# Split weights stored with the columns of eight k-tiles interleaved, in a two-layer encoder on one core

## The chip, the cores and the metric

The kernel runs on one core of one Trainium2 chip. The metric is the device time of one execution in microseconds (us), the median of the runs shown. The engines are PE (matrix multiply; its weight loads are listed apart as PEld), ACT and DVE (elementwise engines), POOL, and SP, which issues the DMAs.

## The reference

The reference is a two-layer encoder over 256 tokens with model width 2048, all in float32. Each layer is a normalisation, a projection to queries, keys and values, attention, an output projection with a residual, a second normalisation and an MLP with squared ReLU of width 8192. Cut to the matrix products, which are nearly all of the work:

```python
# layer 0: w_in (2048 x 6144); layer 1: w_qkv (2048 x 3072)
q, k, v = split(rms_norm(x, g) @ w_in)
x = x + attention(q, k, v) @ w_out                       # w_out (2048 x 2048)
h = rms_norm(x, g2)
a = relu(h @ w1)                                         # w1 (2048 x 8192)
x = x + (a * a) @ w2                                     # w2 (8192 x 2048)
...
return rms_norm(x, g_final)
```

The two attentions (a two-dimensional neighbourhood with dilated windows in layer 0, grouped heads in a band in layer 1) are small beside the products at 256 tokens.

## The kernel before, in words

**Arithmetic.** Each float32 operand of a product is split into two parts in the matmul format `float32r`: a high part `h` (the value rounded to the format) and a low part `l` (what is left). `split(hi, lo, src)` does it: ACT writes the high part (L82), then DVE subtracts it from the source and writes the low part (L83). A product is the sum of high by high, high by low and low by high.

**Tiling.** A weight matrix is cut into units of 128 output columns by 16 k-tiles of 128 rows. A unit comes in two halves of eight k-tiles (`HALF` = 8), each one DMA of 512 KB into a buffer `r` of shape [128, 8, 128] (pool `raw`, six buffers). `take_half()` issues the DMA on SP, splits the half into a tile `h` (pool `whi`) and a tile `l` (pool `wlo`), five buffers each, and runs two halves ahead of their use (`AHEAD` = 2). Both tiles have rows padded to `ROW` = 136 elements, of which 128 are used: k-tile k is a contiguous run of 128 elements, and the next begins 544 bytes further. The instructions at L82 and L83 walk k-tile after k-tile and, inside one, column after column.

**The inner loop.** `k_range` does two matmuls for each k-tile, with the weights as the stationary operand (128x128, read by the weight load) and the activations as the moving one: `h` against 512 elements, which are both parts of the activations side by side (L150), and `l` against the 256 elements of the high part (L152). All go to one accumulator `acc` in PSUM, of which there are three. The moving operand is `u` (normalised input), `o` (attention's output) or `hid` (hidden layer). In the very last unit the 512 elements are taken in two matmuls with 256 each (L147, L148).

**Around it.** Behind a unit, `joined` adds the two halves of the accumulator (ACT L179, DVE L181), and some operations of ACT and DVE on 128x256 follow, which differ by stage. The values of attention (`value_pair`, L272) use weights the other way round: there the activations are stationary and the weights, taken with `flat=True`, are the moving operand. The first unit of the first stage of a group (`some_units`, with `held` > 0) splits the last two k-tiles of a unit into small tiles `hh` and `hl` of their own (pool `held_w`, [128, 2, 128]) and multiplies them later. The first three units of the program (`STARTERS`) are loaded and split in pieces of two or four k-tiles (`GROUPS`) and multiplied at L471 and L473.

The order of the work on each engine is the order in which the code is written; attention's steps are put between the units by a list of due times (`later`, `tick`, every four k-tiles).

Of the kernel before, what the change touches and what calls it, by code (L numbers as in the profile page):

```python
# [8 lines left out]
F32R = mybir.dt.float32r  # L9
# [5 lines left out]
P = 128  # L15
# [9 lines left out]
SCALE = 128.0 ** -0.5  # L25
TW = 384
HALF = KT // 2
ROW = P + 8
RAW_BUFS = 6
PART_BUFS = 5  # L30

# [10 lines left out]
def encoder(ctx: ExitStack, tc: tile.TileContext, a: dict, outT: bass.AP):  # L42
# [4 lines left out]
    whi = ctx.enter_context(tc.tile_pool(name="whi", bufs=PART_BUFS))  # L47
    wlo = ctx.enter_context(tc.tile_pool(name="wlo", bufs=PART_BUFS))
    held_w = ctx.enter_context(tc.tile_pool(name="held_w", bufs=3))
# [31 lines left out]
    def split(hi, lo, src):  # L81
        nc.scalar.activation(hi, src, AF.Copy)  # L82
        nc.vector.tensor_sub(lo, src, hi.bitcast(F32))  # L83
# [6 lines left out]
    def need(units, held=0, flat=False):  # L90

        for i, src in enumerate(units):
            pending.extend([(src[:, :HALF, :], HALF, flat),
                            (src[:, HALF:, :], HALF - 2 if i < held else HALF, flat)])

    def take_half():
        while pending and len(loaded) <= AHEAD:
            src, n, flat = pending.pop(0)
            r = raw.tile([P, HALF, P], F32, name="r")
            nc.sync.dma_start(r, src)  # L100
            h = whi.tile([P, HALF, ROW], F32R, name="h")
            l = wlo.tile([P, HALF, ROW], F32R, name="l")
            if flat:
                h, l = (w.rearrange("p k c -> p (k c)")[:, :HALF * P] for w in (h, l))
                split(h, l, r.rearrange("p k c -> p (k c)"))
                loaded.append((h, l, None))
                continue
            h, l = h[:, :, :P], l[:, :, :P]
            split(h[:, :n, :], l[:, :n, :], r[:, :n, :])
            tiles = [(h[:, k, :], l[:, k, :]) for k in range(n)]  # L110
            if n < HALF:
                h, l = (held_w.tile([P, 2, P], F32R, name=name) for name in ("hh", "hl"))
                split(h, l, r[:, n:, :])
                tiles += [(h[:, k, :], l[:, k, :]) for k in range(2)]
            loaded.append((h, l, tiles))
        return loaded.pop(0)

    def take_unit():
        return take_half()[2] + take_half()[2]
# [65 lines left out]
    def gained(k, which):  # L185
        x, gk = xs[:, k, :], g[:, which, k:k + 1]
        if which == 4:
            nc.scalar.activation(x, x, AF.Copy, scale=gk)
        else:
            nc.scalar.activation(u[:, k, 0, :], x, AF.Copy, scale=gk)  # L190
            nc.vector.scalar_tensor_tensor(u[:, k, 1, :], x, gk, u[:, k, 0, :].bitcast(F32),
                                           op0=ALU.mult, op1=ALU.subtract)
# [68 lines left out]
    def value_pair(pool, keep):  # L261

        ps = acc_ps.tile([P, 2, T], F32, name="acc")
        for half in range(2):
            parts = [take_half()[:2] for _ in range(2)]
            for kk in range(HALF):
                k = half * HALF + kk
                h, l = (w[:, (kk % 4) * T:(kk % 4 + 1) * T] for w in parts[kk // 4])
                for j in range(2):
                    js = slice(j * P, (j + 1) * P)  # L270
                    for n, (x, y) in enumerate(((0, h), (0, l), (1, h))):
                        nc.tensor.matmul(ps[:, j, :], u[:, k, x, js], y,  # L272
                                         start=k == 0 and j == 0 and n == 0,
                                         stop=k == KT - 1 and n == 2, skip_group_check=True)
                if kk % 2 == 1:
                    tick()
        assert norm["ready"]
        w = pool.tile([P, 2, 2, T], F32R, name="v", bufs=1)
        for j in range(2):
            nc.scalar.activation(w[:, 0, j, :], ps[:, j, :], AF.Copy, scale=rcol[:, j:j + 1])  # L280
            nc.vector.scalar_tensor_tensor(w[:, 1, j, :], ps[:, j, :], rcol[:, j:j + 1],
                                           w[:, 0, j, :].bitcast(F32), op0=ALU.mult, op1=ALU.subtract)
        keep.append(w)
# [158 lines left out]
    STARTERS = 3  # L442
# [14 lines left out]
    hl = [None] * STARTERS  # L457
    for k0, k1 in GROUPS:
        ks = slice(k0 % HALF, (k1 - 1) % HALF + 1)
        if k0 % HALF == 0:  # L460
            hl = [(whi.tile([P, HALF, ROW], F32R, name="h")[:, :, :P], wlo.tile([P, HALF, ROW], F32R, name="l")[:, :, :P])
                  for _ in range(STARTERS)]
        for i in range(STARTERS):
            split(hl[i][0][:, ks, :], hl[i][1][:, ks, :], rs[k0 // HALF][i][:, ks, :])
            if i == 0:
                for k in range(k0, k1):
                    gained(k, 0)
        for i in range(STARTERS):
            h, l = hl[i]
            for k in range(k0, k1):  # L470
                nc.tensor.matmul(sps[i], h[:, k % HALF, :], u[:, k].rearrange("p a t -> p (a t)"),  # L471
                                 start=k == 0, stop=False)
                nc.tensor.matmul(sps[i][:, :T], l[:, k % HALF, :], u[:, k, 0, :], start=False, stop=k == KT - 1)  # L473
# [12 lines left out]
    with tc.tile_pool(name="attn0", bufs=1) as pool:  # L486
# [24 lines left out]
        for p in range(8):  # L511
            q, k, v = [[], []], [[], []], []
            for i in range(2):
# [6 lines left out]
                h = 2 * p + i  # L520
# [11 lines left out]
    with tc.tile_pool(name="attn1", bufs=1) as pool:  # L532
        o = pool.tile([P, NH, 2, T], F32R, name="o")
        sl = slopes(16)
        for p in range(2):
            k, v = [[], []], []
# [8 lines left out]
            for i in range(8):  # L545
                h = 8 * p + i
# [93 lines left out]
```

## Time and profile before

| | |
|---|---|
| median of 2 runs | 2112.02 us (2111.78 to 2112.26) |
| the profiled execution, its own time | 2113.29 us |
| its span, first to last instruction | 2111.4 us |
| PE busy | 2088.1 us (99%), 12438 instructions |
| PEld (weight loads) busy | 1846.7 us (87%) |
| DVE busy | 1339.8 us (63%) |
| ACT busy | 1036.6 us (49%) |
| mean granted TensorE clock | 0.995 of full speed |
| DMA | 386 MB, mean 183 GB/s |

A row of a group reads: line, engine, operation, output<-inputs, shapes and types, number of instructions | busy us in total, mean ns of one | idle time of the engine just before them, and what ended it. Matmuls overlap: a matmul's own duration is longer than the distance to the next one, so distances are read from starts in the timeline. PEld runs beside PE.

### The profile page before, as it was taken

To read this page: it belongs to the slowest core of one execution; us is meant where nothing else is said; L and a number is where in the kernel's file an instruction comes from. 1 tells how busy PE (TensorE), PEld (TensorE's weight loads), DVE (VectorE), ACT (ScalarE), POOL (GpSimd) and SP (SyncE) were. 2 spreads that over 40 slices of the span, in tenths; PEclk is the share of its full clock that TensorE was granted. 3 is DMA by queue.
4 is the path that set the end of the run, shared out by engine and by line. 5 is a ranking of instruction groups with operands and counts; after the bars stand their busy time and mean duration, and the time that the engine had idled before them with its cause. 6 is when DMAs were issued, how large, how long until landed. Compare 5 with 4: busy or idle time off the path is not lost.

```text
span 2111.4 us, 31825 instructions
## 1 busy us (share of the span) xinstructions
PE 2088.1 (99%) x12438; PEld 1846.7 (87%) x12438; DVE 1339.8 (63%) x2088; ACT 1036.6 (49%) x1602; POOL 23.0 (1%) x33
## 2 busy tenths in 40 slices
PE   8999999999999999999999999999999999999997
PEld 6999998888888888888889998888888888888887
DVE  6766676666655556666656877766665556665554
ACT  6555555544444444444445656554444434444442
POOL 2100000000000000000000000000000000000000
PEclk9999999999999999999999999999999999999999
DMA  9755555555555555555555454555555555555552
GB/s 260 176 174 167 168 174 174 191 185 189 189 188 189 189 189 189 190 189 190 189 189 185 149 163 144 190 185 188 189 189 189 189 189 189 189 189 190 189 189 91
DMA packets 108294, 386.06 MB, mean 183 GB/s; under 512 B 12352, under 2 KB 13392, under 8 KB 108144
## 3 DMA queue, kind: packets, MB, share of 16 engines
q1 hardware_dynamic: 106992, 381.73, 55.1%
q0 software_dynamic: 1008, 2.27, 1.5%
q8 instruction: 97, 1.59, 0.3%
q14 instruction: 53, 0.43, 0.1%
q10 hardware_dynamic: 144, 0.04, 0.0%
HBM read 381.89 MB, written 2.10 MB: 182 GB/s over the span
## 4 chain that ended last, share of the span: by engine, by line
PE 96%; DMA 2%; DVE 1%; ACT 0%; SPq 0%; issue 0%; DVEq 0%; ACTq 0%
PE acc L150 58%; PE acc L152 30%; PE acc L272 5%; PE s_ps L296 1%; PE m_ps L340 1%; DMA r<-in_even_w_in 1%; PE p_ps L321 1%; DMA r<-in_even_w_v 1%; DMA xs<-in_xT 0%; ACT h L82 0%; DVE l L83 0%; DVE xs L570 0%; PE acc L147 0%; PE acc L148 0%; PE m_ps L225 0%
## 5 line engine op out<-in xcount | busy, mean ns | idle before, releaser
L83 DVE TENSOR_TENSOR l<-r,h 128x1024 fp32r<-128x1024 f32 (+3 forms) x729 | 880.6, 1208 | 701.9 <-ACT h L82 699.3
L82 ACT ACTIVATE h<-r 128x1024 fp32r<-128x1024 f32 (+3 forms) x729 | 762.8, 1047 | 966.0 <-PE acc L150 635.9
L150 PE MATMUL acc<-u,h 128*128 128x512 f32 x2820 | 988.4, 394 | 0.0
L152 PE MATMUL acc<-u,l 128*128 128x256 f32 x2820 | 788.6, 280 | 0.0
L150 PE MATMUL acc<-hid,h 128*128 128x512 f32 x2016 | 702.4, 393 | 0.0
L150 PEld LDWEIGHTS acc<-u,h 128*128 128x128 f32 x2820 | 529.9, 188 | 119.2
L152 PE MATMUL acc<-hid,l 128*128 128x256 f32 x2048 | 572.3, 279 | 0.0
L152 PEld LDWEIGHTS acc<-u,l 128*128 128x128 f32 x2820 | 529.1, 188 | 0.2
L150 PEld LDWEIGHTS acc<-hid,h 128*128 128x128 f32 x2016 | 378.7, 188 | 87.3
L152 PEld LDWEIGHTS acc<-hid,l 128*128 128x128 f32 x2048 | 384.1, 188 | 0.0
L150 PE MATMUL acc<-o,h 128*128 128x512 f32 x500 | 175.2, 394 | 1.1 <-DVE z L181 1.1
L152 PE MATMUL acc<-o,l 128*128 128x256 f32 x500 | 139.8, 280 | 0.0
L272 PE MATMUL acc<-h,u 128*128 128x256 f32 x640 | 119.9, 283 | 0.0
L181 DVE TENSOR_TENSOR z<-acc,t 128x256 f32<-128x256 f32 x275 | 114.4, 418 | 2.2 <-ACT t L179 2.1
L150 PEld LDWEIGHTS acc<-o,h 128*128 128x128 f32 x500 | 93.9, 188 | 22.8 <-DVE z L181 1.7
L179 ACT ACTIVATE t<-acc 128x256 f32<-128x256 f32 x275 | 100.8, 367 | 5.5 <-PE acc L152 2.7
L272 PEld LDWEIGHTS acc<-h,u 128*128 128x128 f32 x640 | 101.1, 190 | 0.5
L152 PEld LDWEIGHTS acc<-o,l 128*128 128x128 f32 x500 | 93.8, 188 | 0.0
L272 PE MATMUL acc<-l,u 128*128 128x256 f32 x320 | 90.1, 281 | 0.0
L272 PEld LDWEIGHTS acc<-l,u 128*128 128x128 f32 x320 | 60.9, 190 | 0.1
L382 DVE SCALAR_TENSOR_TENSOR z<-z 128x256 f32<-128x256 f32 x128 | 54.2, 425 | 4.2
L83 DVE TENSOR_TENSOR hid<-z,hid 128x256 fp32r<-128x256 f32 x128 | 53.5, 419 | 1.3 <-ACT hid L82 1.2
(94 smaller groups left out, 857.6 us busy)
## 6 DMA issues: line engine op xcount, KB each, us to landing
r<-in_w_mlp_in SPq DMA_DIRECT2D x256, 512.0 KB, 4.5
r<-in_w_mlp_out SPq DMA_DIRECT2D x256, 512.0 KB, 4.5
r<-in_even_w_in SPq DMA_DIRECT2D x58, 512.0 KB, 4.2
r<-in_odd_w_qkv SPq DMA_DIRECT2D x40, 512.0 KB, 4.0
r<-in_even_w_v SPq DMA_DIRECT2D x32, 512.0 KB, 3.8
r<-in_even_w_out SPq DMA_DIRECT2D x32, 512.0 KB, 4.2
r<-in_odd_w_out SPq DMA_DIRECT2D x32, 512.0 KB, 3.8
r<-in_odd_w_v SPq DMA_DIRECT2D x8, 512.0 KB, 4.1
```

Of the source, the lines that this page charges most:

```text
L82: nc.scalar.activation(hi, src, AF.Copy)
L83: nc.vector.tensor_sub(lo, src, hi.bitcast(F32))
L150: nc.tensor.matmul(ps, h, act[:, k].rearrange("p a t -> p (a t)"), start=start, stop=False)
L152: nc.tensor.matmul(ps[:, :T], l, act[:, k, 0, :], start=False, stop=stop)
L179: nc.scalar.activation(t, ps[:, T:], AF.Copy)
L181: nc.vector.tensor_add(z, ps[:, :T], t)
L272: nc.tensor.matmul(ps[:, j, :], u[:, k, x, js], y, start=k == 0 and j == 0 and n == 0, stop=k == KT - 1 and n == 2, skip_group_check=True)
L296: nc.tensor.matmul(s_ps[:, i, :], qh[:, x, qs], kh[:, y, :], start=n == 0, stop=n == 2)
L321: nc.tensor.transpose(p_ps[:, j, i * P:(i + 1) * P], s[:, i, j * P:(j + 1) * P], ident)
L340: nc.tensor.matmul(o_ps[:, :T], vv[:, x, j, side * P:(side + 1) * P], pt[:, y, j, :], start=n == 0, stop=n == 5)
L382: nc.vector.scalar_tensor_tensor(z, z, 0.0, z, op0=ALU.max, op1=ALU.mult)
```

## The change

The tiles `h` and `l` of a half become 1024 elements without padding, and the order inside them is turned: element (k, c) stands at c * 8 + k instead of k * 136 + c. The same column of the eight k-tiles lies side by side in 32 bytes; one k-tile is 128 elements with a step of eight elements. The held tiles `hh` and `hl` are laid out the same way for their two k-tiles, with a step of two. Splits still walk k-tile after k-tile and column after column, so ACT writes `h`, and DVE reads `h` and writes `l`, with a step of eight elements; a weight load at L150, L152, L471 and L473 reads with that step. The source `r` is read contiguously as before. The `flat` tiles of the values are contiguous as before. In the built program no instruction is added, removed or moved on any engine (PE 11702 rows, DVE 1835, ACT 1297 in both): only these operands' addresses and steps differ, and the line numbers.

```diff
-ROW = P + 8
...
+    def column_major(pool, n, name):
+
+        return pool.tile([P, P * n], F32R, name=name).rearrange("p (c k) -> p k c", k=n)
...
-            h = whi.tile([P, HALF, ROW], F32R, name="h")
-            l = wlo.tile([P, HALF, ROW], F32R, name="l")
             if flat:
-                h, l = (w.rearrange("p k c -> p (k c)")[:, :HALF * P] for w in (h, l))
+                h, l = (pool.tile([P, HALF * P], F32R, name=name) for pool, name in ((whi, "h"), (wlo, "l")))
...
-            h, l = h[:, :, :P], l[:, :, :P]
+            h, l = column_major(whi, HALF, "h"), column_major(wlo, HALF, "l")
             split(h[:, :n, :], l[:, :n, :], r[:, :n, :])
             tiles = [(h[:, k, :], l[:, k, :]) for k in range(n)]
             if n < HALF:
-                h, l = (held_w.tile([P, 2, P], F32R, name=name) for name in ("hh", "hl"))
+                h, l = (column_major(held_w, 2, name) for name in ("hh", "hl"))
...
-            hl = [(whi.tile([P, HALF, ROW], F32R, name="h")[:, :, :P], wlo.tile([P, HALF, ROW], F32R, name="l")[:, :, :P])
-                  for _ in range(STARTERS)]
+            hl = [(column_major(whi, HALF, "h"), column_major(wlo, HALF, "l")) for _ in range(STARTERS)]
```

## The prediction

> **What bounds the kernel now.** I read the shares of busy time first, then the chain that ended last, then the timeline of the inner loop.
>
> ```profile
> PE 2088.1 (99%) x12438; PEld 1846.7 (87%) x12438; DVE 1339.8 (63%) x2088; ACT 1036.6 (49%) x1602; POOL 23.0 (1%) x33
> ...
> PE 96%; DMA 2%; DVE 1%; ACT 0%; SPq 0%; issue 0%; DVEq 0%; ACTq 0%
> ```
>
> PE is on the path for 96% of the span; DVE and ACT, whose splits the change touches, have 37% and 51% of the span free. So there are two questions: does the new layout alter PE's own step from matmul to matmul, and does it slow the splits so far that DVE or ACT takes PE's place? The groups give the counts and the mean durations.
>
> ```profile
> L150 PE MATMUL acc<-u,h 128*128 128x512 f32 x2820 | 988.4, 394 | 0.0
> L83 DVE TENSOR_TENSOR l<-r,h 128x1024 fp32r<-128x1024 f32 x702 | 860.6, 1226 | 688.7 <-ACT h L82 686.2
> L152 PE MATMUL acc<-u,l 128*128 128x256 f32 x2820 | 788.6, 280 | 0.0
> L82 ACT ACTIVATE h<-r 128x1024 fp32r<-128x1024 f32 x702 | 744.9, 1061 | 946.6 <-PE acc L150 625.2 <-issue 289.5 <-PE acc L272 11.8
> ...
> L152 PE MATMUL acc<-hid,l 128*128 128x256 f32 x2048 | 572.3, 279 | 0.0
> L150 PEld LDWEIGHTS acc<-u,h 128*128 128x128 f32 x2820 | 529.9, 188 | 119.2
> ...
> L152 PE MATMUL acc<-o,l 128*128 128x256 f32 x500 | 139.8, 280 | 0.0
> ```
>
> The rows of L152 count the k-tiles: 2820 + 2048 + 500 = 5368 pairs of one `h` and one `l` matmul (24 pairs on held tiles are left out). No PE row waits. In the timeline of a steady stretch, the columns are start, duration, engine, line:
>
> ```profile
> 999.70 0.39 PE L150 MATMUL acc<-hid,h 128*128 128x512 f32 x1
> ...
> 999.92 0.28 PE L152 MATMUL acc<-hid,l 128*128 128x256 f32 x1
> 999.93 0.19 PEld L150 LDWEIGHTS acc<-hid,h 128*128 128x128 f32 x1
> 1000.04 0.40 PE L150 MATMUL acc<-hid,h 128*128 128x512 f32 x1
> 1000.04 0.19 PEld L152 LDWEIGHTS acc<-hid,l 128*128 128x128 f32 x1
> 1000.27 0.28 PE L152 MATMUL acc<-hid,l 128*128 128x256 f32 x1
> ...
> 1003.88 0.39 PE L150 MATMUL acc<-hid,h 128*128 128x512 f32 x1
> ```
>
> Twelve pairs lie between the starts 999.70 and 1003.88: 0.348 us a pair, and 5368 x 0.348 = 1868 us of the span. Inside a pair, `h` to `l` takes 0.23 us and `l` to the next `h` 0.12 us (0.231 and 0.117 below, so that they add up). Each weight load starts with the matmul before its own (999.93 beside 999.92, 1000.04 beside 1000.04): it is never more than one matmul ahead. So the load of `h` has only the short slot of 0.117 us to hide in. How long a load holds up its matmul is seen where nothing covers it, in the first 10 us:
>
> ```profile
> 8.61 0.19 PEld L471 LDWEIGHTS acc<-u,h 128*128 128x128 f32 x1 [1.51 <-ACT h L82]
> 8.61 0.50 PE L471 MATMUL acc<-u,h 128*128 128x512 f32 x1 [1.19 <-ACT h L82]
> ...
> 9.29 0.39 PE L471 MATMUL acc<-u,h 128*128 128x512 f32 x1
> ```
>
> There load and matmul begin together and the matmul takes 0.50 instead of 0.39 us: the load costs 0.11 us uncovered, call it 0.107, or 0.84 ns for each of 128 columns. With the 0.01 us after which a load starts, 0.107 + 0.01 fills the slot of 0.117. **The load of `h` has no slack at all; the load of `l`, under the long matmul, has 0.231 - 0.117 = 0.114 us.**
>
> **The change part by part.** *Weight loads* (L150, L152 and the starters) read one k-tile with a step of 32 bytes instead of 128 adjacent elements. No weight load of the trace reads with a step, so the cost is bounded. From below it is nothing, less if the two reads of PE hinder each other less than now (a rival below). From above it is the slowest load of the trace, beside one at a granted clock of 0.50:
>
> ```profile
> L439 PEld LDWEIGHTS m_ps<-ones 128*128 128x128 f32 x20 | 4.3, 331 | 1.0 <-DVE eps L73 1.0
> ...
> L471 PEld LDWEIGHTS acc<-u,h 128*128 128x128 f32 x4 | 1.2, 312 | 1.9 <-ACT h L82 1.9
> ...
> 16.00:20.00 4.00, 2.83 (x8) 1.54 (x8) 3.44 (x8) 2.88 (x8) 1.36 (x2) 0.50 1.13 325
> ```
>
> A load takes 124 to 143 ns more than the 188 ns of the inner loop when every column has two of the full clock's steps. I take this as the nearest row to a read that needs a second access for each column, and count the 128 columns alone: +0.107 us a load. Then the load of `h` needs 0.224 us where it had 0.117, all of it exposed: +0.107 us. The load of `l` needs 0.224 us of its 0.231: still covered, by 7 ns. So 5368 x 0.107 = **574 us**. At the upper bound of 0.143 the short slot becomes 0.260 us and the long one 0.260 too, +0.172 a pair or 923 us.
>
> By the Trainium skill, "Advanced Engine Details and Errata", section "Memory Cachelines", SBUF has lines of 16 bytes and wants at least two hits on a line for full speed; every access here goes to another line. No run here shows it yet; the page gives no price, and the sum would be the 574 us above if the penalty is one more access.
>
> *Smaller PE terms.* The starters have 48 such pairs, partly waiting on splits: 48 x 0.107 = 5 us. In the last unit three loads stand in a k-tile instead of two, all in short slots: 32 x 2 x 0.107 = 7 us more. The loads of the values (L272) and of attention keep contiguous operands: nothing.
>
> *Splits.* ACT writes with a step of eight elements, DVE reads `h` and writes `l` with it. The only elementwise read here that isn't forward and contiguous is POOL's, which reads `rev` backwards, rough as POOL's times are:
>
> ```profile
> L505 POOL TENSOR_TENSOR rel<-rev,mask_a x8: 1002/1008/1980, 14.7 to 95.9; 128x384 f32<-128x384 f32 x8
> ```
>
> 1008 ns over 384 elements is 2.6 ns an element, against 1226 / 1024 = 1.2 at L83 and 1061 / 1024 = 1.04 at L82. So a split on DVE costs from 1.23 us (unchanged; there is nothing to gain, its data grow by nothing) to 2.69 us. I take the same second access as for PE, a doubling to 2.45 us. DVE's total is then 1340 + 702 x 1.23 = 2203 us and ACT's at most 1037 + 702 x 1.06 = 1781 us, both below the new span of about 2700. PE's longer pairs hide them: a half of eight k-tiles lasts 8 x 0.455 = 3.64 us instead of 2.78. With that cover gone they cost what the first rival says. Behind a longer split on ACT wait the reads of the accumulator (L179), for at most 1.06 us more, while a unit of 16 pairs takes 7.3 us and three accumulators stand. At the start, where splits come in pieces and nothing covers them, I add 5 us from
>
> ```profile
> L83 DVE TENSOR_TENSOR l<-r,h 128x512 fp32r<-128x512 f32 (+2 forms) x13 | 9.2, 725 | 5.4 <-ACT h L82 5.3
> ```
>
> (9.2 us of these between 14 and 36 us, half of a doubling exposed). Transfers see less demand than now, as a half lasts longer.
>
> *Sum.* 2113.3 (the profiled execution, its span of 2111.4 and 1.9 around it; 1.3 above the median) + 574 + 5 + 7 + 5 = 2704; on the median's scale 2703, rounded to **2700 us**.
>
> **The rivals.** *DVE becomes the bound.* Weight loads take the step free, the splits don't. DVE's slack comes from the windows by stage (PE, PEld, DVE, ACT; ten of them make the sum, and the last row counts the splits of the second):
>
> ```profile
> 60.00:300.00 240.00, 240.00 (x1638) 221.14 (x1638) 165.66 (x300) 127.30 (x226) 9.16 (x10) 1.00 0.56 170
> ...
> 1180.00:1300.00 120.00, 119.91 (x790) 109.14 (x789) 95.14 (x240) 73.07 (x160) 0.00 (x0) 1.00 0.46 150
> ...
> sum 2040.00, PE 2037.86 PEld 1804.21 DVE 1294.38 ACT 1000.50 POOL 9.16; mean PE 203.79 PEld 180.42 DVE 129.44 ACT 100.05 POOL 0.92
> ...
> L83 DVE TENSOR_TENSOR l<-r,h 128x1024 fp32r<-128x1024 f32 x31 | 37.8, 1220 | 11.9 <-ACT h L82 11.9
> ```
>
> 2040 - 1294 = 746 us over 702 splits: DVE takes over once a split costs 1.06 us more (in the second window, layer 1's attention, with 24.9 us for 31 whole splits, from 0.8). Doubled: 702 x 1.23 - 746 = 117, with the start 2235 us; at 2.69 us 702 x 1.46 - 746 = 279, so 2400. Against it: it needs a penalty that strikes DVE and spares PE.
>
> The Trainium skill, "Vector Engine (DVE) Microarchitecture Reference", section "Measured stream behaviour on trn2 (trn3 not measured)", gives 2.50 ns per column for an output with a step of 24 words. An estimate from it: 1024 columns x (2.50 - 1.04) = 1.49 us more a split, 702 x 1.49 - 746 = 300, or about 2420 us. No row here shows a DVE write with a step.
>
> *All of it is hidden.* The matmuls read their moving operand at (394 - 280) / 256 = 0.45 ns a column, the loads at 0.84; so PE's reads can go about twice as fast as a load asks for, and a load with a step may find its time there. If DVE's split also stays under 1.06 us more: 2113 less or more 10.
>
> *Faster.* If loads that sweep the buffer in wide steps collide less with the moving read, the pairs shorten. The spread of the matmuls bounds it:
>
> ```profile
> L150 PE MATMUL acc<-hid,h x2016: 388/393/398, 592.8 to 2086.2; 128*128 128x512 f32 x184
> ...
> L152 PE MATMUL acc<-hid,l x2048: 276/279/288, 593.0 to 2097.8; 128*128 128x256 f32 x187
> ```
>
> Every pair at its shortest saves 5 + 3 = 8 ns, 43 us in all: 2070 us. It decides only if loads cost no more than 0.107 us, since their slot has no slack, and splits no more than 1.06.
>
> *Three accesses a column*, at 0.32 us a load, exposes both loads: 0.33 + 0.33 - 0.348 = 0.312 a pair, 1675 us, about 3800 in all. It would follow from the DVE page's 2.50 ns if PE shared it; the slowest load of this trace speaks against it.
>
> **How the numbers follow.** Chances: weight loads slower and exposed, 2450 to 3060 us: 0.40; DVE the bound, 2160 to 2420: 0.22; hidden, 2075 to 2150: 0.23; faster by over 2%: 0.07; three accesses: 0.08. The first leads because the short slot is full now: any price on a load shows at once, while the splits have 1.06 us in hand. A measurement of this kernel tells about 2% from no change. Faster is 0.07, within 2% 0.23, slower 0.40 + 0.22 + 0.08 = 0.70. The range takes the first three cases, from 2075 to the loads' upper bound, 2113 + 923 + 24 = 3060, and leaves out 0.15. The likeliest case alone has 2450 to 3060.
>
> **What the profile of the changed kernel would show.** Loads at L150 near 295 ns, `l` to `h` near 0.22 us, `h` to `l` still near 0.23, splits near 2.4 us on DVE, DVE around 80% busy and PE still waiting for nothing. The forecast is wrong if loads stay at 188 ns and the pair at 0.348 us: then PE waits for DVE (L83) or nothing has changed. Loads of the held tiles (`hh`, `hl`), with a step of two only, should stay nearer to 188 ns than the others.

## The result, and the profile after

The changed kernel takes 2917.82 us (median of 2 runs, 2915.06 to 2920.57) against 2112.02: a ratio of 1.381, with an interval of 1.378 to 1.384. The forecast was 2700, with a range from 2075 to 3060. The profiled execution's span is 2913.1 us, 801.7 more than before.

The first part of the page and the chain by engine, of the changed kernel (its lines L81, L82, L151, L153 are L82, L83, L150, L152 of before):

```profile
PE 2866.2 (98%) x12438; PEld 2848.7 (98%) x12438; DVE 1987.1 (68%) x2088; ACT 1768.2 (61%) x1602; POOL 25.3 (1%) x33
...
PE 91%; DVE 4%; ACT 3%; issue 1%; DMA 1%; SPq 0%; DVEq 0%; ACTq 0%
```

PE's share hardly moved. What moved is the row beside it: weight loads were busy for 87% of the span and now are for 98%. PE is bound by its loads now, one behind the other without a gap. DVE and ACT are still far from full. The groups, with the shapes kept apart:

```profile
L82 DVE TENSOR_TENSOR l<-r,h 128x1024 fp32r<-128x1024 f32 x702 | 1502.2, 2140 | 843.4 <-ACT h L81 837.2 <-ACT r L214 4.9
L81 ACT ACTIVATE h<-r 128x1024 fp32r<-128x1024 f32 x702 | 1499.8, 2137 | 996.0 <-PE acc L151 672.6 <-issue 308.9 <-PE acc L273 5.8
L151 PE MATMUL acc<-u,h 128*128 128x512 f32 x2820 | 1382.8, 526 | 0.0
...
L153 PEld LDWEIGHTS acc<-u,l 128*128 128x128 f32 x2820 | 965.4, 342 | 0.9 <-DVE l L82 0.8
L151 PEld LDWEIGHTS acc<-u,h 128*128 128x128 f32 x2820 | 921.1, 327 | 0.4
L153 PE MATMUL acc<-u,l 128*128 128x256 f32 x2820 | 818.9, 290 | 0.5 <-DVE l L82 0.5
```

A load went from 188 to 327 (`h`) and 342 ns (`l`), a split from 1226 to 2140 ns on DVE and from 1061 to 2137 on ACT. The 702 splits of a row are not all alike: 40 are those of the values, whose tiles stay contiguous, and they take 1224 ns on DVE and 1060 on ACT here as well. The other 662, with the step, take 2196 and 2202 ns. The stretch of the timeline that answers to the one of before:

```profile
1400.04 0.53 PE L151 MATMUL acc<-hid,h 128*128 128x512 f32 x1
1400.14 0.35 PEld L153 LDWEIGHTS acc<-hid,l 128*128 128x128 f32 x1
1400.40 0.29 PE L153 MATMUL acc<-hid,l 128*128 128x256 f32 x1
1400.40 0.33 PEld L151 LDWEIGHTS acc<-hid,h 128*128 128x128 f32 x1
1400.53 0.52 PE L151 MATMUL acc<-hid,h 128*128 128x512 f32 x1
1400.64 0.34 PEld L153 LDWEIGHTS acc<-hid,l 128*128 128x128 f32 x1
...
1402.97 0.53 PE L151 MATMUL acc<-hid,h 128*128 128x512 f32 x1
```

Six pairs lie between 1400.04 and 1402.97: 0.488 us a pair where it was 0.348. 5368 x 0.140 = 752 us, most of the 802.

The record needs care here. The start of an `h` matmul still stands 0.13 us behind that of the `l` matmul before it, as if its slot had not grown; instead the matmul itself is 526 ns long where it was 394. It begins on record and waits for its weights inside its own duration, as the uncovered matmul of 0.50 us did at 8.61 us of the trace before. Load starts tell the truth: 1400.14, 1400.40, 1400.64, each 0.24 to 0.26 after the last. A load now needs the whole time to the next one, in the short slot and in the long one alike.

### The profile page after: what moved, and what is told of

The parts are those of the page before. It is cut to its first block, busy times and chain, and to the rows that moved or that the text cites. A ratio compares the mean times of both kernels' runs of the same rounds, so it can differ in the third digit from the quotient of the medians.

```text
span 2913.1 us, 31825 instructions
## 1 busy us (share of the span) xinstructions
PE 2866.2 (98%) x12438; PEld 2848.7 (98%) x12438; DVE 1987.1 (68%) x2088; ACT 1768.2 (61%) x1602; POOL 25.3 (1%) x33
## 4 chain that ended last, share of the span: by engine, by line
PE 91%; DVE 4%; ACT 3%; issue 1%; DMA 1%; SPq 0%; DVEq 0%; ACTq 0%
PE acc L151 65%; PE acc L153 23%; DVE l L82 3%; ACT h L81 2%; PE m_ps L341 1%; PE acc L273 1%; PE s_ps L297 1%; DMA xs<-in_xT 0%; PE acc L471 0%; DMA r<-in_even_w_in 0%; PE acc L148 0%; PE acc L149 0%; ACT s L308 0%; PE p_ps L322 0%; DVE v L282 0%
## 5 line engine op out<-in xcount | busy, mean ns | idle before, releaser
L81 ACT ACTIVATE h<-r 128x1024 fp32r<-128x1024 f32 (+3 forms) x729 | 1534.2, 2106 | 1013.3 <-PE acc L151 684.3
L82 DVE TENSOR_TENSOR l<-r,h 128x1024 fp32r<-128x1024 f32 (+3 forms) x729 | 1537.3, 2109 | 855.6 <-ACT h L81 849.4
L151 PE MATMUL acc<-u,h 128*128 128x512 f32 x2820 | 1382.8, 526 | 0.0
L151 PE MATMUL acc<-hid,h 128*128 128x512 f32 x2016 | 986.2, 526 | 0.0
L153 PEld LDWEIGHTS acc<-u,l 128*128 128x128 f32 x2820 | 965.4, 342 | 0.9 <-DVE l L82 0.8
L151 PEld LDWEIGHTS acc<-u,h 128*128 128x128 f32 x2820 | 921.1, 327 | 0.4
L153 PE MATMUL acc<-u,l 128*128 128x256 f32 x2820 | 818.9, 290 | 0.5 <-DVE l L82 0.5
L153 PEld LDWEIGHTS acc<-hid,l 128*128 128x128 f32 x2048 | 704.7, 344 | 0.0
L151 PEld LDWEIGHTS acc<-hid,h 128*128 128x128 f32 x2016 | 657.5, 326 | 0.0
L153 PE MATMUL acc<-hid,l 128*128 128x256 f32 x2048 | 598.2, 292 | 0.0
L151 PE MATMUL acc<-o,h 128*128 128x512 f32 x500 | 246.1, 527 | 4.0 <-DVE z L182 4.0
L153 PEld LDWEIGHTS acc<-o,l 128*128 128x128 f32 x500 | 171.9, 344 | 0.0
L151 PEld LDWEIGHTS acc<-o,h 128*128 128x128 f32 x500 | 163.1, 326 | 5.0 <-DVE z L182 4.6
L153 PE MATMUL acc<-o,l 128*128 128x256 f32 x500 | 146.1, 292 | 0.0
L81 ACT ACTIVATE hid<-z 128x256 fp32r<-128x256 f32 x128 | 55.3, 434 | 9.2 <-DVE z L383 6.4
```

What stands on the lines that cost most here:

```text
L151: nc.tensor.matmul(ps, h, act[:, k].rearrange("p a t -> p (a t)"), start=start, stop=False)
L153: nc.tensor.matmul(ps[:, :T], l, act[:, k, 0, :], start=False, stop=stop)
```

## The experiments

All build on the kernel before. In all but the last two the starters and the held halves (12 of some 700 halves) keep its padded rows, and two helpers name the layouts: `padded` is its own, `column_major` that of the change. Line numbers are their own. Where no interval is given, the run is a single one; runs of the kernel before on the same chip lie within 6 us of each other.

**Which load pays: `h` alone, `l` alone.**

```diff
+            h, l = column_major(whi, "h"), padded(wlo, "l")     # first run
+            h, l = padded(whi, "h"), column_major(wlo, "l")     # second run
```

> Only the high tiles h have the interleaved layout (step of eight); l keeps contiguous rows, as do the starters and the held halves. Loads theory (a stepped weight load needs about 0.235 us for its 128 columns where a contiguous one needs 0.107, and loads are one matmul ahead): the load of h no longer fits under the short matmul, so l to the next h grows from 0.117 to 0.245 us, h to l stays 0.231, 5368 x 0.128 = 687 us more, about 2800 us. Rival, splits theory (the writes and reads of ACT and DVE with a step hold PE up, by late tiles or by the buffer's ports): about half of the change's 806 us, near 2500 us, with pairs lengthened evenly.

> Only the low tiles l have the interleaved layout; h keeps contiguous rows. Loads theory: the load of l has the long matmul to hide under, so h to l grows only from 0.231 to 0.245 us, 5368 x 0.014 = 75 us more, about 2190 us. Splits theory: as much as with h alone, near 2500 us. Even if every stepped load costs PE the same whatever matmul covers it: also about 2500 us.

Measured: 2807.83 us with `h` alone, 2208.99 us with `l` alone, beside 2111.31 for the kernel before on the same chip; 697 and 98 us more, 794 together, where the whole change costs 806. First the groups of the run with `h`, then those of the run with `l`:

```profile
L159 PE MATMUL acc<-u,h 128*128 128x512 f32 x2820 | 1335.1, 516 | 0.0
L159 PEld LDWEIGHTS acc<-u,h 128*128 128x128 f32 x2820 | 889.2, 315 | 120.0 <-ACT h L82 0.2
```

```profile
L159 PE MATMUL acc<-u,h 128*128 128x512 f32 x2820 | 1026.0, 398 | 0.0
L161 PEld LDWEIGHTS acc<-u,l 128*128 128x128 f32 x2820 | 897.5, 318 | 1.2 <-DVE l L83 1.1
```

The loads are equally slow, 315 and 318 ns. The price differs seven times, because one stands under a matmul of 256 columns and the other under one of 512. In the first run `h` matmuls wait (516 ns), in the second they don't (398). From one `h` matmul to the next it is 0.473 us in the first run and 0.361 in the second (medians over the trace; 0.348 before, 0.489 in the change): 671 and 70 us of the 697 and 98 are the pairs. The rest of each is some 27 us that the loads don't explain; both runs also have slower splits. The rivals, by which both runs would be near 2500 us, fall.

**Loads or splits.** In the first run splits write as in the change and loads read contiguous runs; in the second it is the other way round.

```diff
+            h, l = column_major(whi, "h"), column_major(wlo, "l")                                    # first run: write with a step
+            split(h, l, r)
+            h, l = (w.rearrange("p k c -> p (c k)").rearrange("p (k c) -> p k c", c=P) for w in (h, l))  # load contiguously
...
+            split(h, l, r.rearrange("p k c -> p (k c)"))                                             # second run: write contiguously
+            h, l = (w.rearrange("p (c k) -> p k c", k=HALF) for w in (h, l))                         # load with a step
```

> Splits write with a step of eight as in the change, but the weight loads read contiguous runs of 128 elements of the same tiles, so the weights that are multiplied are permuted. Loads theory: PE's pairs stay at 0.348 us; DVE's split is about 2.14 us, 702 x 0.91 = 642 us more busy time against 746 us of slack, so at most waits in attention's stages: 2115 to 2160 us. Splits theory: all of the change, near 2900 us.

> Splits write contiguously as for the values, but the weight loads read with a step of eight elements, so the weights that are multiplied are permuted. Loads theory: nearly all of the change, pairs of 0.49 us, 2112 + 5368 x 0.142 = 2870 us. Splits theory: 2112 us.

Measured: stepped loads alone 2859.65 us, 748 more. Stepped splits alone 2253.07 us, a ratio of 1.068 (1.066 to 1.070), 142 us more: a miss, by some 90 us. The two don't add up (748 + 142 = 890 against 806): the longer pairs cover most of what the splits cost alone, and at most 58 us are left of it, some 5 of them from the starters, which only the change stores with a step. The loads of the second run are those of the change, with its splits back at their old time:

```profile
L162 PEld LDWEIGHTS acc<-u,l 128*128 128x128 f32 x2820 | 959.9, 340 | 0.3
L160 PEld LDWEIGHTS acc<-u,h 128*128 128x128 f32 x2820 | 916.1, 325 | 1.5
L83 DVE TENSOR_TENSOR l<-r,h 128x1024 fp32r<-128x1024 f32 x702 | 860.8, 1226 | 1381.8 <-ACT h L82 1379.8
```

Where the 142 us of the first run went, its groups and windows tell (busy time of PE, PEld, DVE, ACT; the stretch is a part of layer 0's MLP):

```profile
L83 DVE TENSOR_TENSOR l<-r,h 128x1024 fp32r<-128x1024 f32 x702 | 1587.9, 2272 | 165.8 <-ACT h L82 151.2 <-ACT r L223 4.6
...
L83 DVE TENSOR_TENSOR l<-r,h 128x1024 fp32r<-128x1024 f32 x45 | 109.1, 2423 | 3.4 <-ACT h L82 2.5
...
900.00:1030.00 130.00, 128.30 (x704) 107.32 (x703) 125.87 (x111) 113.62 (x89) 0.00 (x0) 1.00 0.51 176
```

In this stretch DVE is busy for 125.9 of 130 us: there it is the bound. And a split takes 2423 ns here, where those with a step average 2336 in this run and 2196 in the changed kernel (2272 and 2140 with the 40 contiguous ones). ACT was busy for 113.6 of the 130 us, in the changed kernel between the same times for 73.8. So a second question came up: do two engines that go through memory with a step slow each other?

```diff
+            h, l = padded(whi, "h"), column_major(wlo, "l")
+            split(h, l, r)
+            l = l.rearrange("p k c -> p (c k)").rearrange("p (k c) -> p k c", c=P)
```

> As the run with stepped splits and contiguous loads, but only the low part l is written with a step; h is written and read contiguously. The loads read contiguous runs, so the low weights that are multiplied are permuted. That run took 142 us more where its expectation had at most 48, with splits of 2.27 us on average. Theory, two engines with stepped accesses at once stretch each other: DVE's split falls to 2.13 to 2.18 us, a unit of the MLP's first product needs 2 x 2.15 + 1.27 = 5.57 us of DVE against 16 x 0.348 = 5.57 us of PE, on the border: 2125 to 2170 us. Rival, DVE is over its limit with one stepped operand as well: splits of 2.25 us and more, 2230 to 2260 us.

Measured: 2146.29 us, 36 more than the kernel before beside it (2110.20).

```profile
L83 DVE TENSOR_TENSOR l<-r,h 128x1024 fp32r<-128x1024 f32 x702 | 1502.8, 2142 | 170.9 <-ACT h L82 164.9
...
900.00:1000.00 100.00, 100.00 (x573) 87.53 (x572) 92.58 (x86) 48.89 (x70) 0.00 (x0) 1.00 0.54 187
```

With ACT contiguous the split is 2142 ns on average instead of 2272, DVE is at 93% in the MLP and PE misses nothing there. That fits the theory that the engines stretch each other. DVE also reads `h` without a step in this run, but that by itself explains little of the difference: in the runs with `h` alone (first) and with `l` alone (second) DVE has one operand with a step, read or written, and a split takes nearly what it takes in the change with both (2140 ns).

```profile
L83 DVE TENSOR_TENSOR l<-r,h 128x1024 fp32r<-128x1024 f32 x702 | 1474.5, 2101 | 778.5 <-ACT h L82 770.8 <-ACT r L222 5.0
```

```profile
L83 DVE TENSOR_TENSOR l<-r,h 128x1024 fp32r<-128x1024 f32 x702 | 1498.1, 2135 | 228.1 <-ACT h L82 223.5
```

In the run with stepped splits alone, the splits with a step that have one of ACT's beside them for over 95% of their time take 2394 ns on average (195 of them), those that have it for under 5% take 2247 (46). What the two engines share was not tried.

**Which steps cost.** Interleaving only two or four k-tiles gives steps of 8 and 16 bytes.

```diff
+            h, l = (pool.tile([P, HALF * ROW], F32R, name=name)[:, :HALF * P].rearrange("p (b c k) -> p b k c", k=2, c=P)   # k=4 in the second run
+                    for pool, name in ((whi, "h"), (wlo, "l")))
+            split(h, l, r.rearrange("p (b k) c -> p b k c", k=2))
...
```

> Only two k-tiles are interleaved: a k-tile has a step of two elements (8 bytes), in splits and loads alike; starters and held halves stay contiguous. Line theory (an access costs more when it goes to another 16 bytes than the one before, and two accesses in 16 bytes are enough): loads near 197 ns as for the change's held tiles, pairs near 0.35 us, splits near 1.23 us, 2110 to 2160 us. Pair theory (full speed only for adjacent elements, the DVE page's rule): splits of 1.8 us and more, loads near 330 ns, as the change, near 2900 us.

> Four k-tiles are interleaved: a step of four elements (16 bytes); starters and held halves stay contiguous. Line theory: every access goes to another 16 bytes, the full price: loads 326 to 344 ns, pairs 0.49 us, splits 2.1 us, near 2880 us. Rival, a price that grows with the step's width: between the kernel before and the change, near 2500 us.

Measured: 2130.43 us with a step of two, 2775.23 us with four, beside 2113.15. The groups of the run with two, then with four:

```profile
L83 DVE TENSOR_TENSOR l<-r,h 128x1024 fp32r<-128x1024 f32 x702 | 862.1, 1228 | 704.9 <-ACT h L82 703.6
L82 ACT ACTIVATE h<-r 128x1024 fp32r<-128x1024 f32 x702 | 799.2, 1139 | 916.8 <-PE acc L160 605.9 <-issue 268.6 <-PE acc L282 12.0
...
L160 PEld LDWEIGHTS acc<-u,h 128*128 128x128 f32 x2820 | 552.8, 196 | 102.0
```

```profile
L82 ACT ACTIVATE h<-r 128x1024 fp32r<-128x1024 f32 x702 | 1412.5, 2013 | 960.2 <-PE acc L160 628.4 <-issue 313.7 <-PE acc L282 9.4
L83 DVE TENSOR_TENSOR l<-r,h 128x1024 fp32r<-128x1024 f32 x702 | 1399.6, 1994 | 818.4 <-ACT h L82 810.1 <-ACT r L223 4.9 <-PE acc L160 1.9
...
L162 PEld LDWEIGHTS acc<-u,l 128*128 128x128 f32 x2820 | 923.5, 327 | 1.7 <-DVE l L83 1.6
L160 PEld LDWEIGHTS acc<-u,h 128*128 128x128 f32 x2820 | 868.5, 308 | 2.0
```

Between a step of 8 and one of 16 bytes stands a cliff, on all three engines: a load goes from 196 to 308 and 327 ns, DVE's split from 1228 to 1994, ACT's from 1139 to 2013. From 16 to 32 bytes (the change) little is added: 327 and 342 ns, 2140, 2137. That agrees with the rule of lines of 16 bytes that need two hits, which the prediction cited from the Trainium skill; that a price grows evenly with the step falls. The loads at 16 bytes are 15 to 19 ns shorter than at 32, so the line isn't quite all of it, and 2775 is 100 us below what I expected. Nor is a step of 8 bytes quite free: ACT's split takes 1139 ns instead of 1061, and the kernel 17 us more, of which the lost padding (below) may be most.

**Is the lost padding a part of it?** The change also drops the padding of the rows.

```diff
-ROW = P + 8
+ROW = P
...
+    const.tile([P, 40], F32, name="shift")     # second run only
```

> Contiguous rows as before, but without the padding (ROW = 128), so that all k-tiles begin at the same place modulo 256 bytes (160). Theory, the address of a load modulo 256 bytes sets its pair's length (in the trace of before k = 0, at 160, has 227 + 118 ns where the mean pair has 348.5): 3.5 ns less a pair, 19 us less, about 2093 us. Rival, the k of the moving operand sets it: no change, 2112 us. The padding's use, on the rival that equal addresses collide: slower.

> As without padding, and 160 bytes of unused memory ahead, so that every k-tile begins at 64 modulo 256 bytes. Theory, the address of a load sets its pair's length (in the trace of before k = 5, at 64, has 226 + 113 ns, the shortest): 9.5 ns less a pair, 51 us less, about 2061 us. Rival, the k of the moving operand sets it: no change, 2112 us.

Measured, medians of five runs each: 2127.61 us without padding (ratio 1.0075, 1.0062 to 1.0087) and 2124.68 us with the shift (1.0057, 1.0043 to 1.0071). My theory that the address modulo 256 bytes alone sets a pair's length is wrong: both are slower, not faster. The padding is worth about 14 us, and what it avoids stays open. At 0.7% it bears no weight in a loss of 38%. No layout tried here beats the kernel before.

## Why the prediction was right, point by point

**The time: short by 218 us, 27% of the 806.** It lies inside the range of the likeliest case, 2450 to 3060. The whole range, from 2075, took in three cases and would have held "hidden" and "DVE becomes the bound" too; that the time fell into it says little. It is the runs that bear the mechanism out.

**The bound and the place: right.** "The load of `h` has no slack at all; the load of `l`, under the long matmul, has 0.114 us" is what the runs with one part alone showed: 697 us for a slower `h`, 98 for an equally slower `l`. "No slack at all" was read from times rounded to 0.01 us and holds to a few ns only: with a step of two elements the loads are 8 ns longer, and 5368 x 0.008 = 43 us more (an estimate) did not come, but 17.

**The size of a load: too small.** The term of 574 us took a second access for each column, +0.107 us a load. From load to load it is 0.244 us now (half of a pair); less the 0.01 us of the start that is 0.234, +0.127. This fails twice. The short slot gives 5368 x 0.127 = 682 us instead of 574. And the load of `l`, which I had covered "by 7 ns", needs 0.244 us of its 0.231: 13 ns over, 70 us where I had none. Together 752, which is the timeline's 0.140 us a pair divided between the two slots. The runs with one part alone measure them apart: 0.125 us more a pair with `h`, 0.013 with `l`. For a load's duration the upper bound, the slowest load of the trace, was the better guide (331 ns, where the new ones have 327 and 342); the sum made from it, 923 us, is as far above 752 as 574 is below.

**Small PE terms and waits.** In the last unit, each of the short matmuls takes 406 ns where it took 281, about as the 7 us assumed (8), and a starter's `h` matmul takes 571 instead of 471, the 5 us assumed for 48 of them. What was missing are PE's waits in attention, where results of DVE come late behind long splits (loads of two attention groups, idle before them in the third part):

```profile
L341 PEld LDWEIGHTS m_ps<-pt,v 128*128 128x128 f32 x192 | 26.7, 191 | 14.7 <-DVE v L282 10.7 <-ACT v L281 2.2 <-DVE pt L82 1.7
...
L297 PEld LDWEIGHTS s_ps<-k,q 128*128 128x128 f32 x192 | 25.8, 189 | 10.3 <-DVE k L82 7.1 <-DVE q L82 2.8 <-ACT k L81 0.3
...
L148 PE MATMUL acc<-hid,h 128*128 128x256 f32 x32 | 13.0, 406 | 0.0
```

The loads of the two attention groups had 1.6 and 1.4 us of idle time before: 22 us more. PE as a whole agrees, with 47 us of its span idle (2913.1 - 2866.2) instead of 23. With 752, 8, 5 and 22 about 15 us of the 802 are not placed.

**Splits: hidden, as said, but for at most 58 us.** I took 2.45 us on DVE; it is 2.20, and ACT has 2.20 where I had 2.12 at most. My sums also counted 702 such splits where 662 have a step; the 40 of the values stay contiguous. DVE is at 68%, not 80%.

**The first rival was cheaper to reach than I had it.** "DVE takes over once a split costs 1.06 us more" divided the slack of all stages by all splits. With loads left alone, 2272 ns on average (1.05 more) already cost 142 us, where the formula gives nothing. The windows of that run fit the reason that slack of one stage does not help another: DVE is busy for 97% of the stretch shown, but for 79% between 60 and 330 us. And a split's time changes with what ACT does beside it.

**"Hidden" and "faster" didn't come.** That the moving operand, which is read contiguously, goes at twice a load's rate did not carry over to a load with a step.

**What I said the profile would show.** Loads near 295 ns: 327 and 342. The slot from `l` to `h` near 0.22 us, `h` to `l` still near 0.23: in the timeline the first stays at 0.13 us and the second grows to 0.36 (1400.04 to 1400.40), since the wait stands inside the `h` matmul. The loads of the held tiles, with a step of two, near 188 ns: yes,

```profile
L151 PEld LDWEIGHTS acc<-u,hh 128*128 128x128 f32 x12 | 2.4, 201 | 0.4
...
L153 PEld LDWEIGHTS acc<-u,hl 128*128 128x128 f32 x12 | 2.4, 197 | 0.0
```

**The cited rules.** With the Trainium skill, "Advanced Engine Details and Errata", section "Memory Cachelines", the runs agree, on PE, ACT and DVE, and give the price that the page lacks. In the Trainium skill, "Vector Engine (DVE) Microarchitecture Reference", section "Measured stream behaviour on trn2 (trn3 not measured)", a step of 24 words takes 2.50 ns per column; here eight words take 1.99 ((2196 - 1226) / 1024 + 1.04, an estimate with the page's 1.04). The same section's rule that full speed needs pairs of adjacent elements does not hold here for DVE: with a step of two no two elements are adjacent, and the split takes 1228 ns instead of 1226.

## What to carry to other kernels

Ask of each weight load which matmul it hides under: a load that is one matmul ahead has that matmul's time, and under 256 columns of this kernel's format there are at most a few ns to spare. Keep float32 weights that are loaded for every matmul contiguous, or at least two elements to 16 bytes; here a step of 32 bytes more than doubled what a load costs (0.107 to 0.234 us), and a split took 1.8 times as long on DVE and 2.1 times on ACT. When a transposed or interleaved layout is needed, put the step where slack is largest, and compute the slack by stage.

## What the runs showed of the hardware

A float32 access with a step of 32 bytes costs about 1 ns more on three engines with different speeds. A weight load of the change spends 0.234 / 128 = 1.83 ns a column, where it had 0.84; ACT's split gained (2202 - 1061) / 1024 = 1.11 ns an element, DVE's (2196 - 1226) / 1024 = 0.95. Whether one limit of the memory stands behind all three was not tried.

DVE's split with a step came out at 2196 ns with ACT contiguous (2142 with the 40 contiguous ones) and at 2423 ns in the MLP with ACT's stepped writes beside it most of the time.

Rows of weights that begin 512 bytes apart cost 0.7% against 544, though a load's own time is the same 188 ns; it shows in the matmuls, 397 ns instead of 394. Whether the distance of the rows or another effect of the smaller buffers does it was not tried. The run without padding:

```profile
L150 PE MATMUL acc<-u,h 128*128 128x512 f32 x2820 | 999.7, 397 | 0.0
...
L150 PEld LDWEIGHTS acc<-u,h 128*128 128x128 f32 x2820 | 529.5, 188 | 126.1
```
